# Three on-chip arenas re-sized by a few words, and what lies where modulo 128 bytes

## The chip, the core and the metric

The kernel runs on one core of one Trainium2 chip. Its engines are TensorE (PE in the profile, with its weight loads listed apart as PEld), VectorE (DVE), ScalarE (ACT), GpSimd (POOL) and the queue of SyncE (SP), which issues most of the transfers. The metric is device time in microseconds (us), lower is better. A run of the kernel before took 1458.84 us, the median of three (1458.84, 1454.71 and 1459.01).

## What is computed

One layer of a hybrid backbone on 1024 latent tokens of width 1024, with a context of 256 tokens. Everything is float32 in and out. Cut to what matters here:

```python
h = _rms(x, lp['norm1']) * (1 + sc1) + sh1
P = _project(h, lp, rope)                 # one input projection for three head groups
o_att = _attend(P['aq'], k_all, v_all)    # 8 query heads, 2 key/value heads
o_dn, _, _ = _bidir_gdn(P, s_f, s_b)      # gated delta rule, one scan per direction
cat = jnp.concatenate([_fourier(P['f']), o_att, dn], axis=-1)   # 256 + 512 + 256 channels
x = x + g1 * (cat @ lp['w_out'])          # output projection, 1024 x 1024
hn = _rms(x, lp['norm2']) * (1 + sc2) + sh2
u = jnp.maximum(hn @ lp['w_ff1'], 0.0)    # 1024 -> 4096
x = x + g2 * ((u * u) @ lp['w_ff2'])      # 4096 -> 1024
```

## The kernel before

**Arithmetic.** A float32 operand of a large product is split into a high part, rounded to the matmul type, and the low rest (`split`: ACT or DVE makes the high part, DVE or GpSimd subtracts). `mm3` (lines 235 to 238) then issues three matmuls for each 128-row step: high by high (L236), high by low (L237), low by high (L238). In a call `matmul(o, l, r)` the operand `l` is the one that is loaded into the array as weights (128 columns), and `r` is the one that is streamed through it, the moving operand.

**Stages, in the order of time in the profiled execution.** Modulations and input projection (to about 240 us), convolutions and the rest of the projections (to 350), attention with the delta-rule scan and the Fourier transform woven into it (to about 709), the output projection (709 to 808), the second norm and the preparation of the feed-forward (808 to 860), the first feed-forward product, FF1 (to 1142), and the second, FF2 (to 1437). FF1 and FF2 use a Strassen form with seven products of halves: FF1 computes for each of 16 column pairs `j` the products 11, 12, s1, s2, s4, s3 and 22, each of four `mm3`, so 12 matmuls of 512 columns.

**Memory.** The kernel hands out on-chip memory by itself. Four big tiles lie in each partition: `fbase` (F, float32, FW words of 4 bytes), `rbase` (R, matmul type, RW words), then on the same side a zone of Z1W words that is given a new name in each stage (`z1a` in the projections, `z1b` in the scan, `z1c` from the output projection to the end of FF1, `z1d` in FF2), and from the other end a zone of Z2W words (`z2a`, `z2b`, `z2c`). F begins at byte 16512, a multiple of 128; R begins where F ends, and Z1 where R ends; Z2 ends at the other end of the memory and begins at byte 190400. `Arena.words` hands out pieces of 64 words and more at multiples of 16 words (64 bytes) within its tile, from the low end or, with `top`, from the high end. `Arena.take` claims a given place.

The remainder of an address modulo 128 is called its residue below. With these sizes F and R begin at residue 0, Z1 and Z2 at residue 64. The operands of the large products are laid out in whole multiples of 128 bytes inside their tiles, so in each of them an operand's residue is that of its tile.

**Who reads what in the stages that the change touches.**

- Output projection: for each of four column blocks (`n4`) and eight row tiles (`q`), eight `mm3` of 256 columns in the order k = 0, 1, 2, 3, 4, 6, 7, 5. The moving operand is the split `w_out` in `z1c`. The weights are `cat(w, k, q)`: the Fourier part (k = 0, 1) and the delta-rule part (k = 6, 7) lie in `z2b`, the attention part (k = 2 to 5) in R. That makes 384 matmuls with weights in R and 384 with weights in Z2.
- FF1: the weights are the split `w_ff1` in `z1c`, the moving operand (512 columns) is a split half of the normed activations. The halves of 11, 12, s2 and s4 and one half of s3 lie in R: 864 matmuls. Those of s1, 22 and the other half of s3 lie in `z2b` (464 matmuls; for 16 more the moving operand is a piece in `z1c` itself).
- FF2: both operands are in R (1344 matmuls of 512 columns).
- Projections: activations in R, split weights in `z1a`, in both roles.

**What sets the order.** The program is written in one sequence, and a scheduler with a model of the times orders it for each engine; every engine then executes its own list strictly in order. `tc.high_priority(n)` moves a piece ahead in that order, and `keep_in_program_order` pins instructions to the written order. The side work `mixing()` (scan, then `spectra()`, which ends with the new `z1c` zone and the buffers of the output projection) is pulled forward step by step between the attention's steps. `values` (L233 with output `bk2`) multiplies the softmax weights by the values; the last three steps of `values` stand next to the first matmuls of the output projection. `w_out` (L1369 ff.) splits a block of the output weights; the first block's low part is made by GpSimd (L1376).

Of the kernel before, what the change touches and what calls it, by code (L numbers as in the profile page):

```python
# [30 lines left out]
NCC = CTX // CK  # L31
NCA = NCL + NCC
EPS = 1e-6
FW, RW, Z1W, Z2W = 16192, 18704, 8576, 9736

COL_F, COL_AQ, COL_AK, COL_DQ, COL_DK, COL_DV, COL_DZ, COL_G = 0, 256, 768, 1024, 1280, 1536, 1792, 2048

# [154 lines left out]
def body(tc, t, out):  # L192
# [3 lines left out]
    with ctx:  # L196
# [4 lines left out]
        def zone(side, n, dt, name):  # L201
            zp = tc.alloc_tile_pool(name=name, bufs=1, side=side, reuse_waits="tile")
            return zp, Arena(zp.tile([P, n], dt, name=name), n)

        zp1, Z1 = zone("left", Z1W, F32R, "z1a")
# [7 lines left out]
        def buf(*shape, top=False, a=None, at=None):  # L213
            return Buf(a or Fa, (P,) + shape, top, at)
# [883 lines left out]
        zp1, Z1 = zone("left", Z1W, F32, "z1b")  # L1098
# [134 lines left out]
        def spectra():  # L1233
# [108 lines left out]

            zp1.release()
            zp1, Z1 = zone("left", Z1W, F32R, "z1c")
            cstb[1].free()
            g1r = [buf(256) for _ in range(2)]
            wb = [buf(4, 256, top=True), buf(4, 256, at=9 * D)] + [rbuf(4, 256, a=Z1) for _ in range(6)]
# [4 lines left out]
        def mixing():  # L1352
            yield from scan()
            yield from spectra()
# [317 lines left out]
        zp1, Z1 = zone("left", Z1W, F32, "z1d")  # L1672
# [131 lines left out]
```

## Time and profile before

| | us |
|---|---|
| runs of the kernel | 1458.84, 1454.71, 1459.01 |
| profiled execution, its time | 1456.26 |
| profiled execution, span of its instructions | 1454.5 |
| PE busy | 1384.1 (95%) |
| DVE busy | 1005.7 (69%) |
| ACT busy | 703.6 (48%) |
| POOL busy | 668.5 (46%) |

The profile's page gives busy times, the span in 40 slices, and the chain of work that ended last. A row of the view by windows gives a stretch of time and for each engine the time it was busy and, behind an x, the instructions that ran in it. Behind the engines stand the granted clock of TensorE, the share of the 16 DMA engines that was busy, and GB/s. A row of the timeline gives the start of an instruction in us from the start of the span, its modelled duration, engine, line, operation, output<-inputs, shapes and a count. Matmuls overlap in their pipeline, so their modelled durations (0.39 us for 512 columns) say little; what counts is the distance from one start to the next, called the pitch below.

### The profile page before, as it was taken

How to read it: one execution, taken by the hardware profiler on the slowest of the kernel's cores; microseconds unless marked ns; L12 is line 12 of the kernel's file. 1: busy time of each engine (PE TensorE's matmuls, PEld its weight loads, DVE VectorE, ACT ScalarE, POOL GpSimd, SP SyncE). 2: the span in 40 equal slices, each digit the busy share in tenths (PEclk: the TensorE clock that was granted, in tenths of full speed). 3: DMA queues.
4: the chain of work that ended last, by engine and by line, in shares of the span. 5: the costliest groups of instructions: out<-in, count | busy, mean ns of one | idle time of the engine just before them, and what ended most of it. 6: DMA issues, size and time to landing. Idle time of an engine off the chain costs nothing.

```text
span 1454.5 us, 28942 instructions
## 1 busy us (share of the span) xinstructions
PE 1384.1 (95%) x11462; PEld 1117.6 (77%) x11462; DVE 1005.7 (69%) x1695; ACT 703.6 (48%) x1239; POOL 668.5 (46%) x739
## 2 busy tenths in 40 slices
PE   4899988989999999989899899999999999999997
PEld 1677977766777777778799777888888888888886
DVE  0774679986878877786633887655556576776984
ACT  1742422323777777776412654554545443443331
POOL 2653679973446466374433733444443100010782
PEclk8999999999999999999999999999999999999999
DMA  8973141242000010042322315544446898766641
GB/s 316 334 257 125 45 118 44 53 93 76 9 10 24 9 38 4 17 142 80 95 84 91 106 55 183 168 147 134 141 151 217 307 392 269 245 230 215 197 157 58
DMA packets 137304, 197.67 MB, mean 136 GB/s; under 512 B 45021, under 2 KB 80463, under 8 KB 136911
## 3 DMA queue, kind: packets, MB, share of 16 engines
q1 hardware_dynamic: 136464, 195.12, 41.0%
q8 instruction: 90, 1.47, 0.4%
q10 hardware_dynamic: 703, 0.69, 0.2%
q14 instruction: 47, 0.39, 0.1%
HBM read 149.84 MB, written 45.94 MB: 135 GB/s over the span
## 4 chain that ended last, share of the span: by engine, by line
PE 47%; DVE 2%; POOL 2%; DMA 1%; issue 1%; ACT 1%; SPq 0%; DVEq 0%; POOLq 0%; ACTq 0%
PE bk L237 8%; PE bk L238 8%; PE bk L236 8%; PE ba L236 7%; PE ba L237 7%; PE ba L238 7%; PE bk L233 1%; DVE z1b L1335 0%; PE ba L233 0%; DMA fbase<-w_out 0%; POOL rbase L1470 0%; DMA fbase<-la 0%; DMA la<-fbase 0%; DVE rbase L998 0%; POOL z2c L1734 0%
## 5 line engine op out<-in xcount | busy, mean ns | idle before, releaser
L220 ACT ACTIVATE rbase<-fbase 128x512 fp32r<-128x512 f32 (+3 forms) x255 | 171.4, 685 | 87.5 <-PE bk L237 54.8
L220 ACT ACTIVATE fbase<-bk 128x512 f32<-128x512 f32 (+3 forms) x224 | 124.9, 561 | 150.8 <-PE bk L233 81.0
L233 PE MATMUL bk<-rbase 128*128 128x256 f32 (+2 forms) x984 | 173.3, 311 | 4.4 <-ACT fbase L220 2.6
L233 PEld LDWEIGHTS bk<-rbase 128*128 128x128 f32 (+1 forms) x984 | 132.3, 175 | 34.1 <-ACT fbase L220 3.4
L220 ACT ACTIVATE z1c<-fbase 128x512 fp32r<-128x512 f32 (+1 forms) x120 | 76.8, 653 | 138.5 <-DMA fbase<-w_ff 51.8
L233 PE MATMUL ba<-rbase 128*65 128x512 f32 (+4 forms) x576 | 138.4, 343 | 5.6 <-DVE rbase L998 4.8
L1503 POOL TENSOR_TENSOR fbase<-fbase 128x512 f32<-128x512 f32 x64 | 87.4, 1366 | 114.4 <-DVE z1c L1470 81.2
L220 ACT ACTIVATE fbase<-fbase 128x512 f32<-128x512 f32 (+4 forms) x148 | 95.9, 659 | 90.6 <-POOL fbase L1626 27.2
L1708 POOL TENSOR_TENSOR z2c<-z2c,fbase 128x512 f32<-128x512 f32 x16 | 31.1, 1969 | 203.8 <-ACT z2c L220 127.9
L974 DVE TENSOR_REDUCE fbase<-ba 128x1 f32<-128x512 f32 (+1 forms) x192 | 106.4, 593 | 19.6 <-PE ba L233 18.3
L220 ACT ACTIVATE rbase<-z1d 128x1024 fp32r<-128x1024 f32 x61 | 63.0, 1055 | 101.9 <-PE bk L237 81.8
L1470 DVE TENSOR_TENSOR z1c<-fbase,z1c 128x512 fp32r<-128x512 f32 x112 | 91.5, 820 | 23.6 <-ACT z1c L220 19.7
L1470 DVE TENSOR_TENSOR rbase<-z1d,rbase 128x1024 fp32r<-128x1024 f32 x61 | 84.9, 1407 | 31.1 <-ACT rbase L220 30.9
L998 POOL TENSOR_TENSOR rbase<-fbase,rbase 128x512 fp32r<-128x512 f32 x56 | 72.1, 1287 | 67.2 <-ACT rbase L220 63.0
L236 PE MATMUL bk<-rbase 128*128 128x512 f32 x256 | 99.7, 389 | 0.0
L237 PE MATMUL bk<-rbase 128*128 128x512 f32 x256 | 99.7, 389 | 0.0
L238 PE MATMUL bk<-rbase 128*128 128x512 f32 x256 | 99.6, 389 | 0.0
L998 DVE TENSOR_TENSOR rbase<-fbase,rbase 128x512 fp32r<-128x512 f32 x104 | 80.5, 774 | 25.7 <-ACT rbase L220 25.3
L1470 DVE TENSOR_TENSOR rbase<-fbase,rbase 128x1024 fp32r<-128x1024 f32 (+1 forms) x65 | 81.0, 1265 | 21.8 <-ACT rbase L220 21.6
L233 PEld LDWEIGHTS ba<-rbase 128*65 128x65 f32 (+1 forms) x576 | 76.2, 155 | 23.3 <-DVE rbase L998 5.9
L238 PE MATMUL ba<-rbase 128*128 128x512 f32 x192 | 74.8, 389 | 0.0
L237 PE MATMUL ba<-rbase 128*128 128x512 f32 x192 | 74.7, 389 | 0.0
(349 smaller groups left out, 3815.8 us busy)
## 6 DMA issues: line engine op xcount, KB each, us to landing
fbase<-w_ff SPq DMA_DIRECT2D x70, 512.0 KB
u<-fbase SPq DMA_DIRECT2D x112, 256.0 KB
z2a<-w_mod SPq DMA_DIRECT2D x36, 512.0 KB
z1d<-w_ff SPq DMA_DIRECT2D x34, 512.0 KB
z1d<-u SPq DMA_DIRECT2D x33, 512.0 KB
fbase<-u SPq DMA_DIRECT2D x23, 512.0 KB
fbase<-w_in SPq DMA_DIRECT2D x16, 512.0 KB
fbase<-x SPq DMA_DIRECT2D x14, 512.0 KB
```

The source lines that it names most:

```text
L220: return SC.activation(o, i, f, **k)
L233: pe(T.matmul(o, l, r, start=start, stop=stop))
L236: pe(T.matmul(o, lh, rh, start=start, stop=False))
L237: pe(T.matmul(o, lh, rl, start=False, stop=False))
L238: pe(T.matmul(o, ll, rh, start=False, stop=stop))
L974: V.tensor_reduce(st4[:, z : z + 1], b, AX.X, ALU.max)
L998: (G if k2 in GP and not any(a <= n < b for a, b in NGP) else V).tensor_tensor(hl[:, :, 1], p, f32(hl[:, :, 0]), op=ALU.subtract)
L1470: eng.tensor_tensor(lo, i, f32(hi), op=ALU.subtract)
L1503: G.tensor_tensor(w[nm], w[a], w[b], op=op)
L1708: G.tensor_tensor(c, c, G2[cs_.start // 512], op=ALU.mult)
```

## The change

FW goes from 16192 to 16176 words and Z1W from 8576 to 8584, and the first 16 words of the zone `z1c` are claimed and not used:

```diff
-FW, RW, Z1W, Z2W = 16192, 18704, 8576, 9736
+FW, RW, Z1W, Z2W = 16176, 18704, 8584, 9736
 ...
             zp1, Z1 = zone("left", Z1W, F32R, "z1c")
+            Z1.take(0, 16)
             cstb[1].free()
             g1r = [buf(256) for _ in range(2)]
             wb = [buf(4, 256, top=True), buf(4, 256, at=9 * D)] + [rbuf(4, 256, a=Z1) for _ in range(6)]
```

F is 64 bytes shorter, so R and Z1 begin 64 bytes lower. The pieces in `z1c` start 64 bytes inside it and so keep their addresses. Z2 stays.

| begins at residue | before | after |
|---|---|---|
| F | 0 | 0 |
| R | 0 | 64 |
| Z1 as `z1a`, `z1b`, `z1d` | 64 | 0 |
| the pieces in `z1c` | 64 | 64 |
| Z2 | 64 | 64 |

Among the matmuls of the matmul type this changes whether the two operands have equal residues for two groups alone: the 864 of FF1 that stream from R, and the 384 of the output projection whose weights lie in R. Both differ before (64 apart) and agree after. Operands of FF2 and of attention lie both in R and move together; those of the projections (R and `z1a`) change places, 0 and 64 before, 64 and 0 after. Pieces at the high end of F lie 64 bytes lower too.

No instruction is added or removed. The scheduler orders some of them differently, all near the end of attention. On PE, whose list there before and after is shown as one piece (bk_78 is the bank of `values`, bk_79 and bk_80 first hold the gate rows, then join the banks ba of the output projection):

```order
 L233 MATMUL bk_80<-fbase 128x256
+L233 MATMUL bk_78<-rbase 65x512
+L233 MATMUL bk_78<-rbase 65x256
+L233 MATMUL bk_78<-rbase 65x512
+L233 MATMUL bk_78<-rbase 65x256
 L236 MATMUL ba_73<-z1c,z2b 128x256
 L236 MATMUL ba_74<-z1c,z2b 128x256
 L236 MATMUL ba_75<-z1c,z2b 128x256
+L236 MATMUL bk_79<-z1c,z2b 128x256
+L236 MATMUL bk_80<-z1c,z2b 128x256
```

One step of `values` now stands ahead of the first matmul of the output projection; the two after it follow closely, where before all three stood 28 to 60 matmuls later. On POOL, at the same place (L998 makes the low part of the softmax weights for `values`, L1338 and L1376 those of the delta-rule output and of `w_out`, L1525 adds a finished block of the output projection to the accumulator; before):

```order
L998 TENSOR_TENSOR rbase<-fbase,rbase 128x2x256
L1338 TENSOR_TENSOR z2b<-z1b,z2b 128x2x256 x2
L998 TENSOR_TENSOR rbase<-fbase,rbase 128x2x256
L1376 TENSOR_TENSOR z1c<-fbase,z1c 128x1024 x2
L998 TENSOR_TENSOR rbase<-fbase,rbase 128x2x256
L1525 TENSOR_TENSOR fbase<-fbase 128x256 x26
```

After (L1377 and L1526 are the former L1376 and L1525):

```order
L1338 TENSOR_TENSOR z2b<-z1b,z2b 128x2x256 x2
L998 TENSOR_TENSOR rbase<-fbase,rbase 128x2x256
L1338 TENSOR_TENSOR z2b<-z1b,z2b 128x2x256
L998 TENSOR_TENSOR rbase<-fbase,rbase 128x2x256
L1377 TENSOR_TENSOR z1c<-fbase,z1c 128x1024 x2
L1526 TENSOR_TENSOR fbase<-fbase 128x256 x26
```

The subtraction that stood behind the two of `w_out` now stands ahead of them.

## The prediction

> **What bounds the kernel now.** I read the page first, to see which engine carries the time, then the view by windows over the stages whose operands change, then the timeline of PE for the pitch.
>
> ```profile
> PE 1384.1 (95%) x11462; PEld 1117.6 (77%) x11462; DVE 1005.7 (69%) x1695; ACT 703.6 (48%) x1239; POOL 668.5 (46%) x739
> PE 47%; DVE 2%; POOL 2%; DMA 1%; issue 1%; ACT 1%; SPq 0%; DVEq 0%; POOLq 0%; ACTq 0%
> ```
>
> The first row is the busy time of each engine, the second the chain of work that ended last, by engine. PE is busy for 95% of the span, and nothing else carries more than 2% of that chain. So the change is worth what it does to PE, stage by stage:
>
> ```profile
> core 0: us, PE busy (x) PEld busy (x) DVE busy (x) ACT busy (x) POOL busy (x), PEclk, DMA share, GB/s
> 709.45:737.00 27.55, 26.90 (x218) 25.72 (x216) 11.19 (x20) 6.79 (x11) 6.70 (x7) 1.00 0.46 144
> 737.00:808.00 71.00, 70.21 (x587) 69.10 (x588) 27.31 (x46) 17.50 (x37) 28.59 (x45) 1.00 0.26 88
> 809.00:860.00 51.00, 45.25 (x201) 34.08 (x200) 46.25 (x64) 32.13 (x58) 22.61 (x20) 0.97 0.21 68
> 860.00:1142.30 282.30, 282.30 (x1217) 227.33 (x1216) 176.16 (x254) 144.02 (x245) 122.15 (x87) 1.00 0.49 164
> 1142.30:1436.00 293.70, 293.70 (x1297) 243.31 (x1297) 213.01 (x173) 117.76 (x124) 65.02 (x33) 1.00 0.70 237
> ```
>
> Rows 1 and 2 are the output projection, row 3 the preparation of the feed-forward, row 4 FF1, row 5 FF2. In FF1, PE is busy all 282.30 us; DVE has 176.16, ACT 144.02, POOL 122.15, the DMA engines half. If PE needs less there, nothing else is near to taking its place. In the output projection PE lacks 27.55 + 71.00 − 26.90 − 70.21 = 1.44 us. Only in row 3 is PE idle (5.75 us) and DVE the busier.
>
> **Does the pitch depend on the residues?** The timeline has the answer for 512 columns. FF1 mixes both kinds of operand within microseconds:
>
> ```profile
> 944.82 0.40 PE L237 MATMUL bk<-rbase,z1c 128*128 128x512 f32 x1
> ...
> 949.48 0.39 PE L236 MATMUL ba<-z2b,z1c 128*128 128x512 f32 x1
> ...
> 953.58 0.40 PE L236 MATMUL ba<-rbase,z1c 128*128 128x512 f32 x1
> ...
> 959.18 0.39 PE L236 MATMUL bk<-z2b,z1c 128*128 128x512 f32 x1
> ...
> 961.92 0.39 PE L236 MATMUL bk<-rbase,z1c 128*128 128x512 f32 x1
> ```
>
> From 944.82 to 949.48 lie 20 matmuls that stream from R (residue 0, weights 64): 4.66 / 20 = 233.0 ns each. Then 18 from `z2b` (64, weights 64): 4.10 / 18 = 227.8. Again 24 from R: 5.60 / 24 = 233.3. Then 12 from `z2b`: 2.74 / 12 = 228.3. Shape, engine, clock and tile of the weights are the same; the source and its residue differ. Two other stages tell whether it is the source:
>
> ```profile
> 271.08 0.39 PE L237 MATMUL ba<-rbase,z1a 128*128 128x512 f32 x1
> ...
> 293.24 0.40 PE L236 MATMUL bk<-rbase,z1a 128*128 128x512 f32 x1
> ...
> 1200.17 0.39 PE L236 MATMUL bk<-rbase 128*128 128x512 f32 x1
> ...
> 1299.91 0.39 PE L238 MATMUL bk<-rbase 128*128 128x512 f32 x1
> ```
>
> In FF2 both operands lie in R and agree: 440 steps in 99.74 us are 226.7 ns. The projection streams from the same R against weights in `z1a` at 64: 95 steps in 22.16 us are 233.3. So R is not slow by itself; it costs 6.6 ns where weights and stream differ by 64.
>
> A rule of the Trainium skill speaks against that reading. Its page SBUF — State Buffer, section "Who interferes with whom", gives PE two read ports, one for the moving operand and one for weight loads, independent of each other, and says that "PE and ACT never wait on anyone". By that rule no residue should cost PE anything, and the change would be worth 0 instead of the terms below; the two pitches above don't agree with it.
>
> **The change part by part.**
>
> *FF1, 864 matmuls from R, 64 apart before, equal after.* Those that run in the stage that PE bounds:
>
> ```profile
> 860.00:1142.30 282.30, 183.84 (x766) 1.00 0.49 164
> ...
> 860.00:1142.30 282.30, 105.07 (x429) 1.00 0.49 164
> ```
>
> These are the window's matmuls with `rbase` (766) and with `z2b` (429). 766 × 6.6 ns = 5.06 us. The runs of `z2b` come out at 227.8 to 228.3 rather than 226.7, since steps between the kinds are longer: 429 × 1.3 = 0.56 us, which goes too when nothing alternates. I take −5.6 us. Bounds: 0 if the pitch isn't a matter of residues, and −6.4 if all 1217 matmuls of the window come to 226.7 (275.9 us for 282.30). The other 864 − 766 = 98 run before 860, where PE is idle for 5.75 us: 98 × 6.6 = 0.65 us covered by DVE's 46.25. Should DVE not cover it, it would be a gain of 0.65 more.
>
> *Output projection, 384 matmuls with weights in R, 64 apart before, equal after.* At 256 columns the trace points the other way:
>
> ```profile
> 743.12 0.28 PE L236 MATMUL ba<-z1c,rbase 128*128 128x256 f32 x1
> ...
> 744.14 0.28 PE L236 MATMUL ba<-z1c,z2b 128*128 128x256 f32 x1
> ...
> 744.86 0.28 PE L236 MATMUL ba<-z1c,rbase 128*128 128x256 f32 x1
> ...
> 166.95 0.28 PE L237 MATMUL ba<-z1a,rbase 128*128 128x256 f32 x1
> ...
> 189.56 0.28 PE L237 MATMUL bk<-z1a,rbase 128*128 128x256 f32 x1
> ...
> 671.50 0.28 PE L236 MATMUL bk<-z2b 128*128 128x256 f32 x1
> ...
> 672.80 0.28 PE L238 MATMUL bk<-z2b 128*128 128x256 f32 x1
> ```
>
> Nine matmuls with weights in R, which differ, take 1.02 us, 113.3 ns each; six with weights in `z2b`, which agree, 0.72 us, 120.0 each. In the first projections 192 that all differ run at 117.8, and 11 steps of the Fourier part that agree at 118.2. So differing is cheaper here only in the neighbourhood of agreeing ones, or for a reason I don't see; agreeing has never been below 118. After the change all 768 agree. If the 384 go from 113.3 to 118.2, the nearest value of an unmixed agreeing run, that is +1.9 us; if to 120.0, +2.6, the upper bound. Lower bound: the `z2b` ones, no longer alternating, come down to 113.3 as well, −2.6. Since some of the stretches with weights in R may already run near 118, as the projections do, I take +1.5.
>
> *The tail of attention.* The pieces of order in the change put one step of `values` ahead of the output projection, two just inside it, and the first matmuls into bk_79 and bk_80 ahead of the lows of `w_out`. The trace of before at that place:
>
> ```profile
> PE ba L233 <- DVE rbase L998: 4.1, 3, 1.9
> ...
> 704.97 2.52 ACT L220 ACTIVATE z1c<-fbase 128x1024 fp32r<-128x1024 f32 x3
> ...
> 706.10 5.18 POOL L1376 TENSOR_TENSOR z1c<-fbase,z1c 128x1024 fp32r<-128x1024 f32 x2
> 711.25 1.47 POOL L998 TENSOR_TENSOR rbase<-fbase,rbase 128x512 fp32r<-128x512 f32 x1
> ...
> 711.60 0.42 DVE L1366 TENSOR_TENSOR fbase<-bk,fbase 128x256 f32<-128x256 f32 x1
> ...
> 713.33 0.91 PE L233 MATMUL bk<-rbase 128*65 128x512 f32 x4
> ...
> L236 PE MATMUL bk<-z1c,z2b 128*128 128x256 f32 x36 | 10.3, 286 | 1.0 <-DVE fbase L1524 1.0
> ```
>
> Now POOL's 1.47 us stand ahead of the 5.18 instead of behind, so the first lows of `w_out`, which L237 of the output projection needs, can come up to 1.5 us later; the highs from ACT (2.52 us) come later too where the exponentials are put ahead of them. PE would stand idle for what `values` doesn't fill (0.91 us a step), and the matmul into bk_79 waits for DVE's gate row (711.60 before, some 2 us after PE's first matmul of this stage). On the other side the waits of 1.0 us for L1524 and for a late `values` can vanish. I take +1.0: two waits of about a microsecond, less what `values` fills. Bounds −1.0 (only the L1524 wait goes) and +4 (two waits like the 1.9 of the first row).
>
> *At nothing.* In the projections the operands change places and stay 64 apart, so 233.3 and 117.8 remain. FF2 moves as a whole and stays equal, 226.7. The scan's zone (`z1b`), FF2's buffers (`z1d`), the pieces at the top of F, and what DVE, ACT, POOL and the DMAs read or write at 64 bytes' offset: in the stages above they are covered by PE, whose shares are 95 to 100%; uncovered, a wait of DVE in row 3 would show at once. I bound these by ±1 us, what PE lacked in the output projection. The 64 bytes left out run no instruction.
>
> Sum: −5.6 + 1.5 + 1.0 = −3.1 us. The profiled execution took 1456.26 us and would take 1453.2. It lies 2.6 below the median of the runs shown, 1458.84, from which the same sum gives 1455.7. I predict from the mean of the four executions, 1457.2: **1454.1 us**.
>
> **The rivals.**
>
> *The residues do nothing on PE*: R against `z1c` would be slow for being two tiles in this arrangement, say by distance. For it speaks that 256 columns go the other way. Against it, `z2b` against `z1c` are two tiles also, farther apart, and run at 227.8. Time: 1457.2 and the tail, so 1457 to 1458. (This is what the rule of the Trainium skill quoted above would give.)
>
> *The gain without the price.* Output projection stays as it was in sum, since the low 113.3 comes from alternation, or the `z2b` ones fall as much as the others rise: −5.6 and a tail of 0 give 1451.6. For it: unmixed runs sit at 117.8 and 118.2 whether they differ or agree; against it, the mean of 113.3 and 120.0 is 116.7, below both.
>
> *Slower: the start of the output projection starves.* PE reaches its first matmuls at about 709.5; if the highs, the lows and the gate rows each come 2 us late in turn, as the 1.9 us waits for L998 did, PE idles 6 us, and with +1.5 it outweighs the 5.6: +1.9, 1459.1. It decides from 4.1 us of waiting on. Against it, POOL's delay is a single 1.47, and `values` fills three times 0.91.
>
> **How the numbers follow.** The forecast has 0.57, the gain without the price 0.18, no effect 0.13, starving 0.12. This kernel's executions differ by 4.3 us, and about 0.3% (4.4 us) is what a measurement can tell from no change; from 1458.84 that border is at 1454.5. The forecast, 1454.1 within its own range of 1451 to 1457.5, lies on it: of its 0.57 I give 0.29 to faster, 0.27 to same. Of the gain without the price 0.15 are faster, of no effect 0.01, of starving 0. Slower by over 0.3% holds only half of the starving, and a little of the others for the spread of the runs. That gives faster 0.45, same 0.47, slower 0.08. The range goes from 1449.5 (the lower bounds of the output projection, halved, under the forecast) to 1459.0 (the starving, which leaves out a part of it).
>
> **What would show it.** Right: in FF1 the runs from R at 226.7 ns like those from `z2b`, its stage about 276.5 us long for 282.3; FF2 still at 226.7 and the projections at 233.3; the weights in R of the output projection at 118 to 120; PE's idle time between 700 and 737 longer by about 1 us. Wrong: R still at 233 in FF1 (then it is no matter of 64 bytes), 113.3 throughout the output projection, or waits of PE for L998, L1366 or L1377 of more than 4 us around 710.

## The result, and the profile after

The changed kernel took 1461.64 us (median of 22 runs, 1457.86 to 1465.88), the kernel before 1457.03 (22 runs, 1453.58 to 1460.2). The ratio is 1.0031, with an interval of 1.0023 to 1.0039: slower by 0.3%, where a gain of 3.1 us was forecast.

The busy times on the page after:

```profile
PE 1390.5 (95%) x11462; PEld 1125.2 (77%) x11462; DVE 1010.5 (69%) x1695; ACT 703.8 (48%) x1239; POOL 668.4 (46%) x739
```

The profiled execution took 1465.88 us and is the longest of the 22. I set the starts of the same matmuls of both traces side by side; how much later they come than before is called the lag. This execution lags by 4.6 us at 688 us already, where all orders are still the same and where another execution with the changed order (below) lags by 0.8; those 4.6 us are no part of the explanation. From 688 to 754 the lag rises by 4.9, from 754 to the start of FF1 by 0.5, in FF1 it falls by 0.5, and in FF2 nothing happens.

FF1 is best read in the view by windows, over the stage from its first matmul to its last, with the matmuls of tile `z1c` alone (before, then after):

```profile
808.60:1142.10 333.50, 316.76 (x1345) 0.99 0.45 149
...
818.70:1151.70 333.00, 316.08 (x1346) 0.99 0.46 150
```

333.5 us before and 333.0 after: the 5.6 us are not there. The timeline of PE in FF1 after shows how the runs from R go now:

```profile
963.83 0.40 PE L238 MATMUL ba<-rbase,z1c 128*128 128x512 f32 x1
964.07 0.39 PE L236 MATMUL ba<-rbase,z1c 128*128 128x512 f32 x1
964.30 0.40 PE L237 MATMUL ba<-rbase,z1c 128*128 128x512 f32 x1
964.54 0.39 PE L238 MATMUL ba<-rbase,z1c 128*128 128x512 f32 x1
...
968.97 0.39 PE L236 MATMUL bk<-z2b,z1c 128*128 128x512 f32 x1
```

From the first row to the last are 22 steps, 5.14 us, 233.6 ns each, as before. Steps are no longer alike: they take turns at 238 and 229 ns. So the 64 bytes did reach these matmuls and changed how they run, but not their mean.

The waits of PE from 690 to 815 us, after:

```profile
PE bk L241 <- DVE z1b L1335: 3.6, 1, 3.6
PE bk L236 <- ACT rbase L220: 2.4, 1, 2.4
PE bk L233 <- DVE rbase L998: 1.5, 2, 1.1
PE ba L233 <- DVE rbase L998: 1.4, 2, 0.7
```

The waits for L998 are smaller than before (4.1 us was their largest row), and two that hardly existed have come: 3.6 us of the transposes for L1335 (0.5 before) and 2.4 us in the output projection (0.2 before). One of 1.0 us for the low of `w_out` (L1377) is new too. This was the rival "the start of the output projection starves", in part.

### The profile page after: what moved, and what is told of

It is laid out like the page before. It is cut to its first block, busy times and chain, and to the rows that moved or that the text cites. A ratio compares the mean times of both kernels' runs of the same rounds, so it can differ in the third digit from the quotient of the medians.

```text
span 1464.0 us, 28942 instructions
## 1 busy us (share of the span) xinstructions
PE 1390.5 (95%) x11462; PEld 1125.2 (77%) x11462; DVE 1010.5 (69%) x1695; ACT 703.8 (48%) x1239; POOL 668.4 (46%) x739
## 4 chain that ended last, share of the span: by engine, by line
PE 48%; DVE 2%; POOL 1%; DMA 1%; ACT 1%; issue 1%; SPq 0%; DVEq 0%; POOLq 0%; ACTq 0%
PE bk L238 8%; PE bk L237 8%; PE bk L236 8%; PE ba L236 8%; PE ba L238 7%; PE ba L237 7%; PE bk L233 1%; PE ba L233 0%; DMA fbase<-w_out 0%; DVE z1b L1335 0%; ACT fbase L220 0%; DMA fbase<-w_ff 0%; POOL rbase L1471 0%; ACT z1c L220 0%; POOL z2c L1735 0%
## 5 line engine op out<-in xcount | busy, mean ns | idle before, releaser
L998 POOL TENSOR_TENSOR rbase<-fbase,rbase 128x512 fp32r<-128x512 f32 x56 | 72.4, 1293 | 71.1 <-ACT rbase L220 67.5
L998 DVE TENSOR_TENSOR rbase<-fbase,rbase 128x512 fp32r<-128x512 f32 x104 | 82.5, 793 | 26.6 <-ACT rbase L220 26.2
```

Source lines behind the costliest of these rows:

```text
L998: (G if k2 in GP and not any(a <= n < b for a, b in NGP) else V).tensor_tensor(hl[:, :, 1], p, f32(hl[:, :, 0]), op=ALU.subtract)
```

## The experiments

Two questions: does the time come from the addresses or from the order (theories A and O), and what must agree for FF1's quick pitch (modulo 128 was wrong: M256, M512, or N, no residue at all). In this program the sizes of the arenas can be changed so that the addresses move and the order stays: words that go from F to R shift R against everything else. Where a list moves with them, it is said.

**r16: the new residues with the old order.**

```diff
-FW, RW, Z1W, Z2W = 16192, 18704, 8576, 9736
+FW, RW, Z1W, Z2W = 16176, 18720, 8576, 9736
```

> Every engine's list is that of before; R begins 64 bytes lower (16 words go from F to R), so FF1's and the output projection's operands stand to each other as in the changed kernel, and the projections' agree modulo 128 too. Theory O (the new order at the end of attention is what costs, the addresses do next to nothing): FF1 about 333 us long as in both kernels, out-projection about 0.5 us longer than before, whole 0 to +1.5 us against before, and no waits of PE like the 3.6 us for L1335 in the changed kernel. Theory A (the addresses themselves cost, in stages besides FF1): +3 to +6 us against before, as the changed kernel.

1456.49 us (12 runs) against 1456.09; ratio 1.0002 (0.9993 to 1.001). No change, so A falls as the cause of the 4.6 us. The run z2off below says so too: but for the pieces in `z1c` it has every address of the changed kernel, in the order of before, and a ratio of 0.9999. FF1 in r16, again the matmuls with `z1c`:

```profile
808.00:1141.10 333.10, 316.13 (x1345) 0.99 0.46 150
```

**ord128: the new order with the old residues.** F is shorter by 512 bytes, which no modulus up to 512 sees, and Z1 has the 8 words more, which are enough for the scheduler to write the changed order: PE's and POOL's lists are those of the changed kernel. DVE's, ACT's and SP's differ from it by four moves earlier than 688 us, which r112 below has as well; there the lag rises by 1.0 us from 688 to 754 us.

```diff
-FW, RW, Z1W, Z2W = 16192, 18704, 8576, 9736
+FW, RW, Z1W, Z2W = 16064, 18704, 8584, 9736
```

> PE's and POOL's lists are those of the changed kernel, but F is 512 bytes shorter than before and nothing is left out in the third zone, so all operands of R, Z1 stand to each other as before modulo 512. Theory O: as slow as the changed kernel, +3 to +6 us against before, PE idle at the end of attention for about 5 us more. Theory A: as before within 1.5 us.

1461.71 us (5 runs) against 1456.09; ratio 1.0039 (1.0027 to 1.0051). Theory O holds: the order alone costs what the change costs. Its lag on before is 0.8 us at 688 us, 5.6 at 754 and at the start of FF1, 5.4 at the end. The waits of PE from 688 to 756:

```profile
PE bk L241 <- DVE z1b L1335: 3.7, 1, 3.7
PE bk L236 <- ACT rbase L220: 2.7, 1, 2.7
PE bk L233 <- DVE rbase L998: 1.4, 2, 0.9
PE ba L237 <- POOL z1c L1376: 1.1, 1, 1.1
PE ba L233 <- DVE rbase L998: 0.7, 1, 0.7
```

With one of 0.2 left out here they come to 9.8 us, against 6.8 us in the same window of before, where the wait for L1335 was:

```profile
PE bk L241 <- DVE z1b L1335: 0.5, 1, 0.5
```

The other 1.7 us of the 4.7 pass while PE is at work, and there its clock is lower. The windows of PE from 698 to 704 and from 704 to 710 us, before and then ord128 (the figure behind PE's busy time and count is the granted clock):

```profile
698.00:704.00 6.00, 3.82 (x24) 1.00 0.01 1
704.00:710.00 6.00, 5.36 (x26) 0.72 0.37 113
...
698.00:704.00 6.00, 5.00 (x20) 0.50 0.07 22
704.00:710.00 6.00, 5.13 (x32) 0.93 0.30 90
```

After the long wait, which ends at 699.0, PE ran at half its clock until about 704.8 (0.93 over six microseconds is 0.50 over the first 0.8 or so). Its 20 matmuls count 5.00 us busy, where 24 counted 3.82 before; the page shows that as work. Before has one such stretch too (the 0.72), and ord128 a second one behind the wait at 731.7 (0.89 over 720 to 736 us).

Why did the wait for L1335 come? The order of DVE, before and in ord128, which the prediction did not look at. In the rows bk_79 and bk_80 are the banks into which PE's transposes (L241) write; L1335 empties them.

```
1001 L998 TENSOR_TENSOR rbase<-fbase,rbase 128x2x256
1002 L1335 TENSOR_TENSOR z1b<-bk_80,z1b 64x2x4x32 x4
1003 L1448 CAST rbase<-fbase 128x128
```

```
1001 L998 TENSOR_TENSOR rbase<-fbase,rbase 128x2x256
1002 L1448 CAST rbase<-fbase 128x128
1003 L1021 TENSOR_TENSOR fbase<-bk_78,fbase 64x256
1004 L1022 TENSOR_TENSOR fbase<-bk_78,fbase 1x256
1005 L998 TENSOR_TENSOR rbase<-fbase,rbase 128x2x256
1006 L1038 TENSOR_TENSOR fbase<-fbase 128x256
1007 L1335 TENSOR_TENSOR z1b<-bk_80,z1b 64x2x4x32 x4
```

Five instructions now stand ahead of L1335 there. In the timeline of DVE (before, then ord128):

```profile
693.12 1.73 DVE L1335 TENSOR_TENSOR z1b<-bk,z1b 64x256 f32<-64x256 f32 x4
...
693.81 1.32 DVE L1448 CAST rbase<-fbase 128x128 fp32r<-128x128 f32 x1
697.12 1.73 DVE L1335 TENSOR_TENSOR z1b<-bk,z1b 64x256 f32<-64x256 f32 x4
```

From 693.12 to 697.12 are 4.0 us, 3.2 more than the lag of 0.8, and PE's next transposes start at 699.00.

The other wait (2.7 us, at 731.7) is the end of a chain that runs through SP's list. The chain of work in ord128 from L1430 on, then of before the issue of the same load, the load, and the matmul at the end:

```profile
714.58 0.34 SPq L1430
714.97 0.50 SPq L1033
715.51 0.60 SPq L1033
716.15 5.87 DMA fbase<-w_out
722.05 1.07 ACT z1c L220
723.14 1.23 DVE z1c L1376
724.40 0.42 DVE fbase L1021
...
725.60 5.06 DMA fbase<-w_ff
730.74 0.63 ACT z1c L220
731.37 0.32 ACT rbase L220
731.73 0.39 PE bk L236
...
711.98 0.42 SPq L1373 DMA_DIRECT2D fbase<-w_out  x1
...
711.98 4.71 DMA fbase<-w_out
...
726.13 0.38 PE L236 MATMUL bk<-z1c,rbase 128*128 128x256 f32 x1 [0.17 <-ACT rbase L220]
```

The load of `w_out` was issued at 711.98 before, ahead of the two of L1033, and at 716.15 here, behind them. Of these 4.2 us, 0.8 are the lag at 688 us, 1.2 the two loads now ahead of it, and 2.2 are there already at L1430 (714.58, before 711.59), which comes behind DVE's work. The load itself took 1.2 us more. Its low part stands on DVE ahead of L1021, which begins the division of the last attention step. The product of the step before that one, which PE needs for k = 5, stands on DVE behind the last step's reciprocal (L1030, at 730.05) and on ACT behind a high of `w_ff1` (730.74).

Before, PE waited 0.17 us for that product: the chain had no slack. Here it ends 5.6 us later, 4.8 past the lag of 0.8, and that is what PE loses between 688 and 754 us. So I read the loss as this chain's; no run puts SP's old order back into the changed one. GpSimd's low of the first block (L1376) ran from 706.10 before and from 711.90 here, 5.8 us later where the prediction allowed 1.5.

**u1: one thing less ahead of L1335.** The changed kernel, with a copy moved from DVE to GpSimd; PE's list stays that of the changed kernel.

```diff
-        V.tensor_copy(idb(), C["ident"])
+        G.tensor_copy(idb(), C["ident"])
```

> The changed kernel with one copy of 128 columns (L1448, 1.3 us on DVE at the end of attention in the run ord128) given to GpSimd; PE's list is that of the changed kernel. It stood on DVE between PE's transposes and the products L1335 that PE then waited 3.65 us for. Theory Q (what DVE has ahead of L1335 sets that wait): the wait falls by up to 1.3 us, whole 0.5 to 2 us under the changed kernel, +3 to +4 us against before. Theory P (DVE waits there for PE or POOL anyway): the wait stays at 3.5 to 3.7 us.

1460.8 us (12 runs) against 1457.37; ratio 1.0025 (1.0013 to 1.0036). L1335 starts at 695.05, and PE's row for these transposes is now

```profile
696.92 0.64 PE L241 MATMUL bk<-fbase,z1b 128*128 128x128 f32 x4 [2.76 <-POOL rbase L998]
```

2.76 us for 3.65: the wait follows DVE's list, as theory Q says. The view names GpSimd's L998 as the releaser; DVE's L1335 is the work that ended last here. But the loss at the end of attention didn't shrink with it: from 688 to 754 us the lag rises by 4.9 us in u1 as in the changed kernel. The wait in the output projection took it back, with 3.0 us for 2.4:

```profile
PE bk L236 <- ACT rbase L220: 3.0, 1, 3.0
```

The load of `w_out` was issued earlier here (713.97), but took 6.73 us, against 5.87 in ord128; whether that is chance, one profile can't tell. In the whole, the gain on the changed kernel (1.0025 for 1.0031, intervals overlap) is inconclusive.

**r48 and r112: which modulus.** More words from F to R, in the same line: 16144 and 18752 in r48, 16080 and 18816 in r112.

> 48 words go from F to R: moving operand and weights of FF1's products from R are 256 bytes apart modulo 512 (before 448, in the changed kernel 384). Theory M256 (they have to agree modulo 256): these 864 matmuls come down from 233.3 to 226.7 ns a step, FF1 about 5 us shorter. Theory M512 (they have to agree modulo 512): 233 ns, nothing in FF1. Theory N (no matter of residues, but of the two tiles): 233 ns too.

> 112 words go from F to R: they are 0 bytes apart modulo 512. M256 and M512: 226.7 ns a step, FF1 5 to 6 us shorter than before, the output projection's 384 matmuls with weights in R at 118 to 120 ns (+0.5 to +2 us), projections of 512 columns at 226.7 instead of 233.3 too (480 of them, up to -3 us where PE bounds); whole 4 to 8 us faster than before. Theory N: 233 ns, whole as before within 1.5 us.

r48: 1453.65 us (9 runs) against 1456.09, ratio 0.9977 (0.9967 to 0.9986). r112: 1454.3 (11 runs), ratio 0.9986 (0.9976 to 0.9997). FF1 in r48 and in r112, then two stretches of r48's timeline:

```profile
809.50:1136.90 327.40, 310.38 (x1346) 0.99 0.46 152
...
811.80:1139.40 327.60, 310.11 (x1346) 0.99 0.46 152
...
952.16 0.39 PE L236 MATMUL ba<-rbase,z1c 128*128 128x512 f32 x1
...
957.60 0.39 PE L236 MATMUL bk<-z2b,z1c 128*128 128x512 f32 x1
...
960.32 0.39 PE L236 MATMUL bk<-rbase,z1c 128*128 128x512 f32 x1
```

24 matmuls from R in 5.44 us and 12 from `z2b` in 2.72: 226.7 ns for both. FF1 is 6.1 us shorter than before in r48, 5.9 in r112. At this width agreement is what counts, and it is agreement modulo 256: r48 is 256 apart modulo 512, r112 is 0 apart, and they run alike. M512 and N fall. In the whole r48 gains 2.4 us, as the output projection pays for it (120.0 ns a step for 117.2 in the table below, some 2 us over its 768 matmuls). The page on SBUF in the Trainium skill (SBUF — State Buffer, "Who interferes with whom") would have PE wait on nobody; between r16 and r48 the place of R differs (and one earlier load in SP's list), and FF1 differs by 5.7 us; the measurement decides.

r112 gains 1.8 us in the whole, where 4 to 8 were expected, and less than r48 with the same FF1; with F that much shorter, DVE's, ACT's and SP's lists differ a little from before's, and FF1 began 2.3 us later in its profile than in r48's. What each of these costs isn't shown.

**r40: 32 bytes apart** (16152 and 18744).

> 40 words go from F to R: operands of FF1's products from R are 32 bytes apart modulo 256. If a pitch of 226.7 ns needs the very same residue modulo 256, they stay at 233 and FF1 at 333; if a coarser unit than 32 bytes decides, they come to 226.7 and FF1 to 327.5. By M256 as the runs with 64, 128 and 192 bytes have it, the former is likelier.

1458.97 us (12 runs) against 1456.96; ratio 1.0014 (1.0002 to 1.0026). FF1:

```profile
811.00:1144.60 333.60, 316.46 (x1345) 0.99 0.46 150
```

No gain at 32 bytes either. DVE's and SP's lists have one move each against before's, so the 0.14% of the whole need not be the addresses'.

**z2off: agreement taken away** (only FW changes, to 16176).

> Only F is 64 bytes shorter; every engine's list is that of before. R and z1c move together, so FF1's products from R stand as before (448 apart modulo 512), but those from z2b, which agreed, are now 64 bytes apart, and so are the 384 of the output projection with weights in z2b. Theory M256: FF1's 464 matmuls from z2b rise from 227 to 233 ns, FF1 about 2.5 to 3 us longer; the output projection, in which now all 768 differ, at about 117.7 ns like the first projections, within 1 us of before; whole +2 to +3.5 us. Theory N (tiles, not residues): nothing changes.

1456.76 us (12 runs) against 1456.96; ratio 0.9999 (0.999 to 1.0009), where 2 to 3.5 us more were expected.

```profile
805.50:1139.80 334.30, 317.10 (x1346) 0.99 0.45 149
```

FF1 is 0.8 us longer than before, not 2.5 to 3: the matmuls from `z2b` rose from 228.4 to 229.2 ns in the mean, not to 233. So 64 bytes apart (as here) is cheaper than 192 apart (as R before) at this width, and the runs of `z2b` in before were not all at 226.7 to start with. The gain came from elsewhere: the output projection ran at 113.6 ns a matmul (190 steps in 21.58 us), where 117.7 was expected.

**best1 and best2: FF1 agreeing, the output projection not.** Both have r48's sizes and its gain in FF1. In best1 the buffers of `z1c` are 1088 words apart and the output projection uses them from word 16 on; best2 also moves its weights in `z2b` by 32 words, and gives these words back at the end of the stage.

```diff
-            ... + [rbuf(4, 256, a=Z1) for _ in range(6)]
+            ... + [rbuf(1088, a=Z1) for _ in range(6)]
 ...
-                h, l = hi(None, (P, 4, 256)), lo(None, (P, 4, 256))
+                h, l = view(hi, 16, 4, 256)(), view(lo, 16, 4, 256)()
```

```diff
-            zp2, Z2 = zone("right", Z2W, F32R, "z2b")
+            zp2, Z2 = zone("right", Z2W, F32R, "z2b"); Z2.take(0, 32)
```

> As r48 (FF1 agrees modulo 256), and the split w_out stands 16 words further in z1c, in buffers 1088 words apart, so that all 768 matmuls of the output projection differ by 64 bytes modulo 128. Theory M256: FF1 stays at 327.4 us; the output projection's pitch falls from 119.8 in r48 to about 117.7 ns, 1.6 us; whole 1.6 us under r48, about 4 us under before. If differing is dear at 256 columns too, it is no faster than r48.

> As best1, and the Fourier and delta-rule parts (the output projection's weights in z2b) stand 128 bytes further, so that its moving operand is 64 bytes ahead of the weights in R and 192 ahead of those in z2b modulo 256, the pattern that ran at 114.0 ns in z2off. FF1 still agrees. If the pattern of residues alone sets the pitch: 114 ns instead of 117.6, 768 x 3.6 = 2.8 us under best1, some 8 us under before. If something else made z2off's output projection quick, as best1.

best1: 1450.86 us (6 runs) against 1456.96, ratio 0.9963 (0.995 to 0.9977). best2: 1451.04 (6 runs) against 1457.37, ratio 0.9951 (0.9936 to 0.9966). Both beat the kernel before, and so the changed one; the intervals do not tell them from each other. The pitch of the output projection is read from one stretch of 190 steps, which ran without a pause in all of these kernels: its first and last row in before, r16, r48, best1 and best2.

```profile
760.14 0.28 PE L237 MATMUL ba<-z1c,z2b 128*128 128x256 f32 x1
782.40 0.28 PE L238 MATMUL bk<-z1c,rbase 128*128 128x256 f32 x1
...
759.21 0.28 PE L237 MATMUL ba<-z1c,z2b 128*128 128x256 f32 x1
781.74 0.28 PE L238 MATMUL bk<-z1c,rbase 128*128 128x256 f32 x1
...
760.16 0.28 PE L237 MATMUL ba<-z1c,z2b 128*128 128x256 f32 x1
782.96 0.28 PE L238 MATMUL bk<-z1c,rbase 128*128 128x256 f32 x1
...
760.20 0.28 PE L237 MATMUL ba<-z1c,z2b 128*128 128x256 f32 x1
782.58 0.28 PE L238 MATMUL bk<-z1c,rbase 128*128 128x256 f32 x1
...
759.10 0.28 PE L237 MATMUL ba<-z1c,z2b 128*128 128x256 f32 x1
780.68 0.28 PE L238 MATMUL bk<-z1c,rbase 128*128 128x256 f32 x1
```

The second column gives the address of the moving operand less that of the weights, modulo 256, for weights in R and for weights in `z2b`:

| kernel | R / `z2b` | us | ns a step |
|---|---|---|---|
| before | 64 / 0 | 22.26 | 117.2 |
| r16 | 128 / 0 | 22.53 | 118.6 |
| r48 | 0 / 0 | 22.80 | 120.0 |
| best1 | 64 / 64 | 22.38 | 117.8 |
| best2 | 64 / 192 | 21.58 | 113.6 |

At 256 columns agreeing is the dearest of the five, the reverse of 512 columns. best2's pattern of residues took 21.58 us for the same 190 steps in z2off too, in another placement of everything; so the pattern sets it. Of the 2.8 us expected under best1, 2.3 are there at the start of FF1 in the profiles (2.28 us ahead of before for best2, 0.06 behind for best1).

## Why the prediction was wrong

*FF1, −5.6.* Measured −0.5 in the changed kernel. The step that failed is "it costs 6.6 ns where weights and stream differ by 64": the rows of before held only pairs 0 and 64 apart modulo 128, and I took the modulus from the change, not from a row. Modulo 256 the quick pairs of the trace (FF2, `z2b`) were at 0 and the slow ones at 192; the change moved the slow ones to 128, which is no better. The size was right: at 0 modulo 256 FF1 is 6.1 us shorter (r48), 5.5 of them in the part from 860 us on that the forecast of 5.6 was for. I could have seen the question in the addresses of the pieces, had I written the differences down to more than 128.

*Output projection, +1.5.* The direction held, by luck. In r16, whose operands there stand as in the changed kernel, in before's order, the stretch above went from 117.2 to 118.6 ns, 1.1 us if all 768 matmuls go like it. The forecast was 0.4 too dear. The reason given, that agreeing costs 118 to 120, again had the wrong modulus: the 384 matmuls went to 128 apart, and a real agreement is r48's 120.0.

*The tail, +1.0, bounds −1.0 to +4.* Measured +4.7 in ord128 between 688 and 754 us, outside the bounds. Here the step was the choice of the lists: I read PE's and POOL's and priced what moved in them, but the largest new wait comes from DVE's list (L1335 behind five others), and the second ends a chain through DVE's and SP's (the load of `w_out` behind L1033), which comes 4.8 us late. That chain is what the loss hangs on, as far as the traces show: u1 cut the first wait by 0.9 us and the loss stayed. Nor did the sum hold what a wait of 3.7 us does to the clock of the work behind it. The rival that named starving had the right sign and place, but not this cause; it counted on 4.1 us of waits to outweigh FF1's gain, and 3.0 more came, with 1.7 of slower work, while that gain did not.

*At nothing.* Right as far as can be told: FF2 kept its pace, and in r16 the projections agree modulo 128 without any gain in the whole.

The sum by measured terms: −0.5 in FF1, +1.1 in the output projection and +4.7 in the tail are +5.3, against +4.6 between the medians. The lower end of the range, 1449.5, doesn't follow from the bound that it names: −2.6 for +1.5 is 4.1 us less, which gives 1450.0, and halved 1452.0. Not settled: why 8 words more in Z1 let the scheduler write another order.

## What to carry to other kernels

An edit to sizes or addresses alone can write another order; compare the lists of all engines and of SP's queue, and try the addresses and the order apart, as r16 and ord128 do. A rule on residues wants rows on both sides of each modulus that it might have: write the differences of address out modulo 256 and more before you choose. And a placement that suits one product's width can be wrong for the next, so place each stage's operands by their own pitch.

## What the runs showed of the hardware

For matmuls of 512 columns the pitch was 226.7 ns where moving operand and weights have the same address modulo 256 bytes (FF2 in before, FF1 in r48), and about 233 in FF1 where they are 32 (r40), 128 (r16, the changed kernel) or 192 apart (before); at 64 apart (z2off) it was 229 in the mean. For 256 columns the same address gave 120.0 ns (r48), 64 apart 117.8 (best1), and 64 and 192 in turn 113.6 (best2, z2off). Why two differences in turn can be quicker than one alone stays open (64 and 0 in turn gave 117.2 in before, under both); no run has 192 alone.

After 3.66 us without work PE's granted clock was 0.50 for nearly 6 us of work in ord128, and after 3.65 us in the changed kernel for 3.4; four transposes took 1.09 us in both instead of 0.62. In u1 a wait of 2.76 us was enough for 3.4 us at 0.50.
